# Delta rule layer: convolution sums partly in PSUM, substitution on blocks of 16 with a merge to 32 on TensorE, and compact factors for the merges

## The chip, the cores and the metric

One core of a Trainium2 chip runs the whole program. The metric is device time in microseconds (us) of one execution. TensorE (PE) does the matmuls, VectorE (DVE), ScalarE (ACT) and GpSimd (POOL) the elementwise work, and SyncE (SP) issues the DMAs.

## The reference

The network has two layers: an even one (state-space mixer and neighbourhood attention) and an odd one (gated delta rule), each with an MLP, over 128 prompt and 512 sample tokens of width 1024. The change touches the odd layer alone:

```python
def _deltanet_mixer(h, s0, w_in, conv_w, a_log, dt_bias, norm_g, w_out):
    proj = h @ w_in
    qkv = silu(_dwconv(proj[..., :3 * D_MODEL], conv_w))      # 5 taps along the tokens
    ...
    q = q * rsqrt(sum(q * q) + EPS) * DN_DK ** -0.5           # 8 heads of 128
    k = k * rsqrt(sum(k * k) + EPS)
    o_f, s_f = _gdn_chunked(q, k, v, g[:, :, 0], beta[:, :, 0], s0[:, 0])
    o_b, s_b = _gdn_chunked(q[:, ::-1], k[:, ::-1], ...)      # backward direction
    o = _rmsnorm(o_f + o_b[:, ::-1], norm_g) * silu(z)
    return o @ w_out, ...

def _gdn_chunked(q, k, v, g, beta, s0):
    a_mat = tril_strict((kb @ k.T) * decay)
    t_mat = triangular_solve(eye + a_mat, eye)                # inverse of a unit triangle
    u_c, w_c = t_mat @ (v * beta), t_mat @ (kb * exp(gcum))
    def step(s, xs):                                          # chunk after chunk
        v_new = u_i - w_i @ s
        o = (q_i * exp(g_i)) @ s + at_i @ v_new
        s = s * exp(g_last) + (k_i * exp(g_last - g_i)).T @ v_new
```

## The kernel before, in words

Features lie on the 128 partitions and the 640 tokens along the free axis. A matrix product of the network is `gemm`: for each 128 outputs it takes 2 halves of 320 tokens, and for each of the 8 input tiles three matmuls (lines 205 to 207: the weight split into a high part `whi` and a low part `wlo`, the input likewise), 24 matmuls to a half. ACT makes `whi` (line 194), POOL the difference `wlo` (line 196).

The odd layer (`odd`) works on pairs of heads, four of them. For each pair:

1. `gdn_project` runs a gemm of six output tiles m (k of two heads, q of two heads, v of two heads). Its function `ev` copies each half to a buffer `cb` (tag `cb`, two buffers; the prompt's 128 and the sample's 512 tokens with zeros between), and after the second half does the convolution on one tile `cv` of 642 columns: ACT writes the first tap (line 1319), DVE adds the four others (line 1322), ACT takes the tanh (line 1328), and a product gives silu (lines 1335 and 1336 on DVE; for the two q tiles lines 1331 to 1333 on ACT and POOL). For the v tiles of pairs 1 to 3 the last tap is done by ACT and POOL (lines 1325 and 1326). `squares` (line 1272), `tok` (line 1299) and `normalize` (line 1285) then send `cv` through TensorE, each into a PSUM bank of the tag `pc`, which has two banks.
2. `gdn_group`, for each of 5 chunks of 128 tokens, builds the triangles of two heads and two directions and writes them to DRAM (`ud`). Their 32x32 diagonal blocks, 80 of them, are gathered in a tile `ub`, one block on each of 80 partitions.
3. `gdn_blocks` inverts the 80 blocks in place by 31 substitution steps on DVE, each a product (line 1425) and a subtraction (line 1427). The result goes to DRAM (`dd`).
4. `gdn_inverse` reads it back (`gcm`), spreads it by a mask on POOL (line 1453) to block-diagonal 128x128 tiles `gD` and, transposed on DVE (line 1454), `gTT`; then merges 32x32 to 64x64 to 128x128 inverses by small matmuls (line 1458) with 128 rows and 32 or 64 columns, and ACT copies between.
5. `gdn_chain` runs the recurrence over the chunks: lines 1615, 1625, 1631, 1632 and 1643 are its matmuls of each step, 1620 and 1646 its DVE steps, and line 1567 multiplies the decayed q on POOL.

In the code a pair's steps 4 and 5 stand after the next pair's projection, with a higher priority; the last pair's stand beside the gemm of z (`zproj`, its `ev` at lines 1721 to 1724). A scheduler of the framework sets the order on each engine from these priorities when the program is built; each engine then runs its list in order, and waits on semaphores. After the layer come modulation vectors (line 281), the gating of the outputs (`gated`) and the output gemm.

Of the kernel before, what the change touches and what calls it, by code (L numbers as in the profile page):

```python
# [20 lines left out]
T = 640  # L21
# [127 lines left out]
class Build:  # L149
# [1098 lines left out]
    def gdn_project(self, pr, hn, P, first=None, mid=None):  # L1248
# [45 lines left out]
        def tok(ty):  # L1294
            for part in range(3):
# [7 lines left out]
                if part < 2:  # L1303
                    nc.scalar.activation(dst[part][:, 1:5], pv, AF.Copy)
                else:
                    for hh in range(2):
                        V.tensor_copy(dst[hh][:, 0], pv[:, hh])
        def ev(m, h, p):
# [9 lines left out]
            cv = self.tl([128, 642], "cv")  # L1318
            nc.scalar.activation(cv, cb[m][:, 0:642], AF.Identity, scale=cw[:, 0:1])  # L1319
            split = m > 3 and pr > 0  # L1320
            for t in range(1, 4 if split else 5):
                V.scalar_tensor_tensor(cv, cb[m][:, t:t + 642], cw[:, t:t + 1], cv, op0=M, op1=AD)  # L1322
            if split:
                cy = cb[m][:, 4:646]
                nc.scalar.activation(cy, cy, AF.Identity, scale=cw[:, 4:5])
                nc.gpsimd.tensor_tensor(cv, cv, cy, op=AD)
            th = cb[m][:, 0:642]
            nc.scalar.activation(th, cv, AF.Tanh)

            if m in (2, 3):  # L1330
                nc.scalar.activation(th, th, AF.Identity, bias=1.0)
                nc.gpsimd.tensor_tensor(cv[:, 0:128], th[:, 0:128], cv[:, 0:128], op=M)
                nc.gpsimd.tensor_tensor(cv[:, 128:T], th[:, 130:642], cv[:, 130:642], op=M)
            else:
                V.scalar_tensor_tensor(cv[:, 0:128], th[:, 0:128], 1.0, cv[:, 0:128], op0=AD, op1=M)
                V.scalar_tensor_tensor(cv[:, 128:T], th[:, 130:642], 1.0, cv[:, 130:642], op0=AD, op1=M)
# [78 lines left out]
    def gdn_blocks(self, pr, ub, P):  # L1415

        nc = self.nc
        V = nc.vector
        D = ub
        V.memset(D.rearrange("p a b -> p (a b)")[:, 0:1024:33], 1.0)  # L1420
        tmp = P.tile([80, 256], F32, name="sbt", bufs=1)
        for j in range(31):
            n, m = 31 - j, j + 1
            t = tmp[:, :n * m].rearrange("p (a b) -> p a b", b=m)
            V.tensor_tensor(t, ub[:, j, j + 1:32].unsqueeze(2).to_broadcast([80, n, m]),
                            D[:, j, 0:m].unsqueeze(1).to_broadcast([80, n, m]), op=ALU.mult)
            V.tensor_tensor(D[:, j + 1:32, 0:m], D[:, j + 1:32, 0:m], t, op=ALU.subtract)
            if j < 30:
                tmp = P.tile([80, 256], F32, name="sbt", bufs=1)
        dd = self.dp.tile([20, 4, 1024], F32, name="dd", tag="dd", bufs=2)  # L1430
        nc.sync.dma_start(out=dd.rearrange("a b c -> (a b) c"), in_=D.rearrange("p a b -> p (a b)"))
        return dd

    def gdn_inverse(self, pr, ud, dd, P):
# [3 lines left out]
        cm = P.tile([128, 20, 32], F32, name="gcm")  # L1438
        nc.sync.dma_start(out=cm, in_=self.ap(dd, 0, [[32, 128], [4096, 20], [1, 32]]))
# [5 lines left out]
        mask = self.cst[:, 404:532].rearrange("p (b j) -> p b j", b=4).unsqueeze(1).to_broadcast([128, 2, 4, 32])  # L1445

        D = P.tile([128, 5, 4, 128], F32, name="gD")
        TT = P.tile([128, 5, 4, 128], F32, name="gTT", bufs=2)
        two = lambda t, c, d: t[:, c, 2 * d:2 * d + 2].rearrange("p u j -> p (u j)")
        for c in range(5):  # L1450
            for d, a, b in ((0, D, TT), (1, TT, D)):
                src = cm[:, 4 * c + 2 * d:4 * c + 2 * d + 2].unsqueeze(2).to_broadcast([128, 2, 4, 32])
                G.tensor_tensor(a[:, c, 2 * d:2 * d + 2].rearrange("p u (b j) -> p u b j", b=4), src, mask, op=ALU.mult)
                V.transpose(two(b, c, d), two(a, c, d))
        CH = [(c, hh) for c in range(5) for hh in range(2)]

        def mm(out, l, r, col):
            nc.tensor.matmul(out, l, r, start=True, stop=True, tile_position=(0, col))

        def bank(n):  # L1460
            return self.ps("pb")[:, :320].rearrange("p (c h j) -> p c h j", c=5, h=2)


        p = bank(0)
        for c, hh in CH:
            for a in (0, 64):
                x, y = slice(a, a + 32), slice(a + 32, a + 64)
                mm(p[y, c, hh], uo[:, 0, c, hh, a:a + 32], D[:, c, hh, x], a + 32)
                mm(p[x, c, hh], uo[:, 1, c, hh, a:a + 32], D[:, c, 2 + hh, y], a)
        X = cm[:, :10].rearrange("p (c h) j -> p c h j", c=5)  # L1470
        ACT.activation(X, p, AF.Copy)
        pD, pT = bank(0), bank(0)
        for c, hh in CH:
            mm(pD[32:64, c, hh], TT[:, c, hh, 32:64], X[:, c, hh], 32)
            mm(pD[64:96, c, hh], TT[:, c, 2 + hh, 64:96], X[:, c, hh], 64)
        ACT.activation(D[32:64, :, 0:2, 0:32], pD[32:64], AF.Copy, scale=-1.0)
        ACT.activation(D[64:96, :, 2:4, 96:128], pD[64:96], AF.Copy, scale=-1.0)
# [11 lines left out]
        Y = cm.rearrange("p (c h a) j -> p c h (a j)", c=5, h=2)
        parts = ((0, 4), (4, 5))  # L1490
        for c0, c1 in parts:
            p = self.ps("pb").rearrange("p (c h j) -> p c h j", c=4, h=2)
            for c in range(c0, c1):
                for hh in range(2):
                    mm(p[y, c - c0, hh], uo[:, 0, c, hh, 32:96], D[:, c, hh, x], 64)
                    mm(p[x, c - c0, hh], uo[:, 1, c, hh, 0:64], D[:, c, 2 + hh, y], 0)
            ACT.activation(Y[:, c0:c1], p[:, :c1 - c0], AF.Copy)
        for c0, c1 in parts:
            p = self.ps("pb").rearrange("p (c h j) -> p c h j", c=4, h=2)
            for c in range(c0, c1):  # L1500
                for hh in range(2):
                    mm(p[x, c - c0, hh], Y[:, c, hh], TT[:, c, hh, y], 0)
                    mm(p[y, c - c0, hh], Y[:, c, hh], TT[:, c, 2 + hh, x], 64)
            ACT.activation(TT[x, c0:c1, 0:2, y], p[x, :c1 - c0], AF.Copy, scale=-1.0)
            ACT.activation(TT[y, c0:c1, 2:4, x], p[y, :c1 - c0], AF.Copy, scale=-1.0)
# [16 lines left out]
    def gdn_chain(self, pr, pd, TT, P, roles, bank):  # L1522
# [14 lines left out]
        def load(c):  # L1537

            if c not in held:
# [3 lines left out]
                held[c] = [a[k][:, i] for k in range(2) for i in range(4)]  # L1543
# [454 lines left out]
```

## Time and profile before

| what | value |
|---|---|
| median of 3 runs | 1980.04 us (1975.23 to 1983.87) |
| profiled execution | 1976.35 us, of which the span from first to last instruction is 1974.1 us |
| PE busy | 1799.6 us, 91% of the span |
| DVE busy | 1290.8 us, 65% |
| ACT busy | 869.5 us, 44% |
| POOL busy | 760.8 us, 39% |
| mean granted TensorE clock | 0.963 of full speed |

Busy time is the union of an engine's instruction spans; the odd layer takes about 900 to 1470 us of the span. The granted clock is a mean over the two levels of TensorE, 1.2 and 2.4 GHz, so 0.91 of a stretch means that a part of it ran at the lower level. Two of the profile's views are used by stretch: busy time of each engine, and the waits of an engine with what ended them.

### The profile page before, as it was taken

The page shows a single profiled execution, that of the slowest core. Times are in us where ns is not written, and L with a number is a line of the kernel's source. Part 1 is how long each engine was busy: PE and PEld are TensorE (multiplying, and loading weights), DVE is VectorE, ACT ScalarE, POOL GpSimd, SP SyncE. Part 2 cuts the span into 40 slices and gives each one's busy share as a digit, 9 for nine tenths or more (in the row PEclk, how much of TensorE's full clock was granted, in tenths as well). Part 3 has the DMA queues.
Part 4 walks back from the last instruction along what each step waited for, and adds up shares of the span by engine and source line. Part 5 has one row for each costly group of instructions (what it writes and reads, how often), then busy time and mean ns, then how long its engine had stood idle before and what let it go on. Part 6 is the DMA issues. An engine that isn't in the chain of part 4 may idle for free. (4 is left out here: it accounts for less than half of the span.)

```text
span 1974.1 us, 35755 instructions
## 1 busy us (share of the span) xinstructions
PE 1799.6 (91%) x13556; PEld 1698.3 (86%) x13556; DVE 1290.8 (65%) x2825; ACT 869.5 (44%) x1928; POOL 760.8 (39%) x609
## 2 busy tenths in 40 slices
PE   5889889998999999998877889889989899999998
PEld 3789677988999999998877788787878899999997
DVE  8999777369264544548589988774667927364553
ACT  4333356344244353536454455344324425344362
POOL 2622101442343433453455555522235334343451
PEclk9999999998999999998998999898989999999999
DMA  8446886524332222332576478758834122222231
GB/s 319 131 112 169 239 246 228 195 106 140 124 112 84 76 86 75 135 123 78 158 207 196 117 197 238 222 166 267 279 131 149 54 97 76 86 76 86 76 96 54
DMA packets 206985, 286.61 MB, mean 145 GB/s; under 512 B 54879, under 2 KB 138237, under 8 KB 206813
## 3 DMA queue, kind: packets, MB, share of 16 engines
q1 hardware_dynamic: 206812, 284.33, 45.6%
q8 instruction: 107, 1.75, 0.4%
q14 instruction: 66, 0.53, 0.1%
HBM read 228.87 MB, written 46.82 MB: 140 GB/s over the span
## 5 line engine op out<-in xcount | busy, mean ns | idle before, releaser
L196 POOL TENSOR_TENSOR wlo<-raw,whi 128x1024 fp32r<-128x1024 f32 (+1 forms) x153 | 360.8, 2361 | 512.6 <-ACT whi L194 466.6
L194 ACT ACTIVATE whi<-raw 128x1024 fp32r<-128x1024 f32 (+1 forms) x153 | 153.2, 1002 | 324.5 <-PE pg L206 146.6
L207 PE MATMUL pg<-hidh,wlo 128*128 128x320 f32 (+2 forms) x576 | 178.8, 311 | 0.5 <-POOL wlo L196 0.5
L205 PE MATMUL pg<-hidh,whi 128*128 128x320 f32 (+2 forms) x576 | 179.0, 311 | 0.0
L206 PE MATMUL pg<-hidl,whi 128*128 128x320 f32 (+2 forms) x576 | 178.9, 311 | 0.0
L205 PE MATMUL pg<-h10h,whi 128*128 128x320 f32 x472 | 158.9, 337 | 17.5 <-DVE cb L1722 6.5
L422 DVE SCALAR_TENSOR_TENSOR x<-pg,mod,x 128x128 f32<-128x128 f32 (+2 forms) x132 | 53.7, 436 | 179.5 <-PE pg L207 179.5
L206 PE MATMUL pg<-h10l,whi 128*128 128x320 f32 x472 | 155.9, 330 | 0.0
L207 PE MATMUL pg<-h10h,wlo 128*128 128x320 f32 x472 | 155.3, 329 | 0.0
L205 PE MATMUL pa<-hidh,whi 128*128 128x320 f32 x448 | 138.0, 310 | 0.5 <-ACT whi L194 0.5
L207 PE MATMUL pa<-hidh,wlo 128*128 128x320 f32 x448 | 138.4, 309 | 0.0
L206 PE MATMUL pa<-hidl,whi 128*128 128x320 f32 x448 | 138.2, 309 | 0.0
L422 DVE SCALAR_TENSOR_TENSOR x<-pa,mod,x 128x128 f32<-128x128 f32 (+2 forms) x108 | 43.8, 435 | 136.8 <-PE pa L207 136.8
L507 POOL TENSOR_TENSOR wq<-S,wq 128x512 fp32r<-128x512 f32 x52 | 71.3, 1371 | 114.4 <-ACT wq L506 114.4
L205 PEld LDWEIGHTS pg<-h10h,whi 128*128 128x128 f32 x472 | 95.9, 203 | 21.4 <-DVE cb L1722 7.2
L207 PEld LDWEIGHTS pg<-hidh,wlo 128*128 128x128 f32 x576 | 108.2, 188 | 1.6 <-POOL wlo L196 1.0
L205 PEld LDWEIGHTS pg<-hidh,whi 128*128 128x128 f32 x576 | 108.3, 188 | 0.9 <-issue 0.8
L206 PEld LDWEIGHTS pg<-hidl,whi 128*128 128x128 f32 x576 | 108.2, 188 | 0.4 <-DVE hidl L568 0.3
L1322 DVE SCALAR_TENSOR_TENSOR cv<-cb,cw,cv 128x642 f32<-128x642 f32 x90 | 94.6, 1052 | 9.8 <-ACT cv L1319 8.9
L206 PEld LDWEIGHTS pg<-h10l,whi 128*128 128x128 f32 x472 | 95.9, 203 | 0.6 <-issue 0.4
L207 PEld LDWEIGHTS pg<-h10h,wlo 128*128 128x128 f32 x472 | 95.6, 203 | 0.2
L205 PEld LDWEIGHTS pa<-hidh,whi 128*128 128x128 f32 x448 | 83.9, 188 | 2.0 <-ACT whi L194 1.2
(742 smaller groups left out, 5754.2 us busy)
## 6 DMA issues: line engine op xcount, KB each, us to landing
raw<-in_wff SPq DMA_DIRECT2D x104, 512.0 KB
mraw<-in_wmod SPq DMA_DIRECT2D x96, 512.0 KB
raw<-in_wino SPq DMA_DIRECT2D x33, 512.0 KB
rawx<-in_wff SPq DMA_DIRECT2D x24, 512.0 KB
raw<-in_wine SPq DMA_DIRECT2D x16, 512.0 KB
cka<-pd SPq DMA_DIRECT2D x28, 256.0 KB
ckb<-pd SPq DMA_DIRECT2D x28, 256.0 KB
s5g<-s5g SPq DMA_DIRECT2D x32, 164.0 KB
```

The source lines that it names most:

```text
L194: nc.scalar.activation(hi[:, :kt], raw[:, :kt], AF.Copy)
L196: (nc.vector if self.lov and self.nw % self.lov else nc.gpsimd).tensor_tensor(lo[:, :kt], raw[:, :kt], hi[:, :kt], op=ALU.subtract)
L205: nc.tensor.matmul(p[:, :n], hi[:, k], xh[:, s], start=(k == 0), stop=False)
L206: nc.tensor.matmul(p[:, :n], hi[:, k], xl[:, s], start=False, stop=False)
L207: nc.tensor.matmul(p[:, :n], lo[:, k], xh[:, s], start=False, stop=(k == kt - 1))
L422: nc.vector.scalar_tensor_tensor(x[m][:, s], p[:, ls], g, x[m][:, s], op0=ALU.mult, op1=ALU.add)
L507: (V if j % 2 else nc.gpsimd).tensor_tensor(t[:, 4:8], src, t[:, 0:4], op=SU)
L1322: V.scalar_tensor_tensor(cv, cb[m][:, t:t + 642], cw[:, t:t + 1], cv, op0=M, op1=AD)
```

## The change

- The convolution is a function `conv`. The prompt's 128 columns stay in `cv`; the sample's 512 columns are summed in a PSUM bank of the tag `pc`. Every step is done twice, once for each part. The products of the q tiles and the last tap of the v tiles go from POOL and ACT to DVE, for all pairs.
- The substitution works on blocks of 16: 15 steps, each on the two 16x16 diagonal blocks of a 32x32 block at once, into a tile `ubd` of its own that POOL clears. `ub` has one buffer in place of two.
- The pieces are read back compactly: `gDc` and `gTc` (32 rows on each of four partition groups), `gGc` (the 16x16 off-diagonal pieces, zero elsewhere), in 4 + 8 DMAs a pair in place of one. A first merge from 16 to 32 is new: two rounds of 80 matmuls of 32x32 with tile positions of row and column (line 1463), an ACT copy, a subtraction and two transposes on DVE. The later merges use the same compact factors: matmuls read 32 or 64 rows in place of 128. ACT copies the pieces to `TT` and `D64`, which POOL clears. The mask on POOL and the 40 transposes on DVE are gone.
- In the chain the decayed q is multiplied by DVE, two products of 256 columns in place of four of 128 on POOL.
- Buffers after the layer take tags that still exist (`gTT`, `gDc`), and the modulation weights alternate between `ub` and `ubd`.

```diff
+        def conv(x, cw):
+            cv = self.tl([128, 642], "cv")
+            cl = self.ps("pc")
+            parts = ((cv[:, 0:128], 0), (cl, 130))
+            for o, c0 in parts:
+                nc.scalar.activation(o, x[:, c0:c0 + o.shape[1]], AF.Identity, scale=cw[:, 0:1])
+            for t in range(1, 5):
+                for o, c0 in parts[::-1]:
+                    V.scalar_tensor_tensor(o, x[:, c0 + t:c0 + t + o.shape[1]], cw[:, t:t + 1], o, op0=M, op1=AD)
+            for o, c0 in parts[::-1]:
+                nc.scalar.activation(x[:, c0:c0 + o.shape[1]], o, AF.Tanh)
+            for (o, c0), c1 in zip(parts[::-1], (128, 0)):
+                V.scalar_tensor_tensor(cv[:, c1:c1 + o.shape[1]], x[:, c0:c0 + o.shape[1]], 1.0, o, op0=AD, op1=M)
+            return cv
...
+            cv = conv(cb[m], cw)
...
-        for j in range(31):
-            n, m = 31 - j, j + 1
...
+        D = P.tile([80, 32, 32], F32, name="ubd", bufs=1)
+        nc.gpsimd.memset(D, 0.0)
+        nc.gpsimd.memset(D.rearrange("p a b -> p (a b)")[:, 0:1024:33], 1.0)
+        def both(t, i, n, j, m):
+            return bass.AP(tensor=t.tensor, offset=t.offset + 32 * i + j, ap=[list(t.ap[0]), [528, 2], [32, n], [1, m]])
+        for j in range(15):
+            n, m = 15 - j, j + 1
+            sh = [80, 2, n, m]
+            t = P.tile([80, 128], F32, name="sbt", bufs=1)[:, :2 * n * m].rearrange("p (s a b) -> p s a b", s=2, b=m)
+            V.tensor_tensor(t, both(ub, j, 1, j + 1, n).rearrange("p s a b -> p s b a").to_broadcast(sh),
+                            both(D, j, 1, 0, m).to_broadcast(sh), op=ALU.mult)
+            V.tensor_tensor(both(D, j + 1, n, 0, m), both(D, j + 1, n, 0, m), t, op=ALU.subtract)
...
-                G.tensor_tensor(a[:, c, 2 * d:2 * d + 2].rearrange("p u (b j) -> p u b j", b=4), src, mask, op=ALU.mult)
-                V.transpose(two(b, c, d), two(a, c, d))
...
+        V.transpose(fl(Tc[:, 0]), fl(Dc[:, 0]))
+        V.transpose(fl(Dc[:, 1]), fl(Tc[:, 1]))
+        def mm(out, l, r, row, col):
+            nc.tensor.matmul(out, l, r, start=True, stop=True, tile_position=(row, col))
...
+        for d in range(2):
+            for n in range(10):
+                for r in S:
+                    mm(px[d][r, n], Gc[r, d, n], Dc[r, d, n], r.start, r.start)
+            ACT.activation(Xc[:, d], px[d], AF.Copy)
+        px = [bank() for d in range(2)]
+        for d in range(2):
+            for n in range(10):
+                for r in S:
+                    mm(px[d][r, n], Tc[r, d, n], Xc[r, d, n], r.start, r.start)
+            V.tensor_tensor(Dc[:, d], Dc[:, d], px[d], op=ALU.subtract)
+            V.transpose(fl(Tc[:, d]), fl(Dc[:, d]))
+        G.memset(D64, 0.0)
+        G.memset(TT, 0.0)
...
-                for u in range(4):
-                    nc.gpsimd.tensor_tensor(gq[:, u], gq[:, u], lds[u][2 + u % 2], op=M)
+                for d in range(2):
+                    V.tensor_tensor(gq[:, 2 * d:2 * d + 2], gq[:, 2 * d:2 * d + 2], lds[2 * d][8], op=M)
```

Since the scheduler lists every engine anew, the order moves as well. On DVE, where the substitution of the first pair begins, the list before holds the full-width steps of `cv` and the growing steps on `ub` (a row is line, operation, output<-inputs, shape):

```order
L1425 TENSOR_TENSOR sbt<-ub 80x31
L181 TENSOR_TENSOR l2n_t<-l2n_t,l2n_h 128x10
L1427 TENSOR_TENSOR ub<-ub,sbt 80x31
L182 SCALAR_TENSOR_TENSOR l2n_y<-l2n_t,l2n_y 128x10
L1425 TENSOR_TENSOR sbt<-ub 80x60
L1278 TENSOR_TENSOR ktok<-ktok,l2n_y 128x640 x2
L1427 TENSOR_TENSOR ub<-ub,sbt 80x30x2
L1425 TENSOR_TENSOR sbt<-ub 80x87
L1322 SCALAR_TENSOR_TENSOR cv<-cb,cw,cv 128x642
L1427 TENSOR_TENSOR ub<-ub,sbt 80x29x3
```

and after the change the same place on DVE holds the halved blocks and the split convolution:

```order
L1428 TENSOR_TENSOR sbt<-ub,ubd 80x30
L1322 SCALAR_TENSOR_TENSOR cv<-cb,cv 128x128
L1318 SCALAR_TENSOR_TENSOR pc<-cb,cw,pc 128x512
L1430 TENSOR_TENSOR ubd<-ubd,sbt 80x2x15
L1428 TENSOR_TENSOR sbt<-ub,ubd 80x56
L1430 TENSOR_TENSOR ubd<-ubd,sbt 80x2x14x2
L1428 TENSOR_TENSOR sbt<-ub,ubd 80x78
L1318 SCALAR_TENSOR_TENSOR cv<-cb,cw,cv 128x128
L1430 TENSOR_TENSOR ubd<-ubd,sbt 80x2x13x3
```

The steps on blocks end at 128 elements where they ended at 256, and the convolution's 642 columns have become 512 and 128. On PE the merges of the first pair stand behind 594 of the 1968 matmuls of the layer's gemms (before: behind 921), with the new level in front:

```order
L1463 MATMUL pb<-gDc,gGc 32x32 x40
L1463 MATMUL pb<-gXc,gTc 32x32 x80
L1272 MATMUL pc<-cst,tsq 128x2
L1463 MATMUL pb<-gDc,guf 32x32
L1272 MATMUL pc<-cst,tsq 128x2 x2
L206 MATMUL pg<-h10l_8974,whi 128x320
L207 MATMUL pg<-h10h_8973,wlo 128x320
L205 MATMUL pg<-h10h_8975,whi 128x320
```

The last pair's chain begins on PE behind 1704 of these matmuls, where it began behind 1584, so that 96 of them stand beside it, where 208 did, and in its last step no gemm is left between its matmuls. Before, the last step on PE reads

```order
L1625 MATMUL pb<-cR,gTT 128x128 x4
L1631 MATMUL pb<-cgq,cS 128x128
L205 MATMUL pg<-ozh_15958,whi 128x320
L206 MATMUL pg<-ozl_15959,whi 128x320
L207 MATMUL pg<-ozh_15958,wlo 128x320
```

and with the change

```order
L291 MATMUL pc<-cst,mrow 128x128 x2
L1674 MATMUL pb<-cR,ckd 128x128 x4
L1646 MATMUL pb<-cS,cka 128x128 x4
L1656 MATMUL pb<-cR,gTT 128x128 x4
L1662 MATMUL pb<-cgq,cS 128x128
L1663 MATMUL pb<-cbc,cR 128x128
```

so the matmuls of the output gemm that stood inside the step (15 of them before its second part) have moved out of it.

## Rows read from the trace of the kernel before

**Rows 1.** Busy time by engine in the layer's three stretches, then PEclk, DMA.
```profile
900.00:1000.00 100.00, 85.44 (x554) 83.63 (x553) 71.42 (x107) 55.17 (x111) 47.59 (x59) 0.91 0.47 146
1000.00:1250.00 250.00, 210.49 (x1855) 200.51 (x1853) 226.80 (x475) 129.15 (x293) 143.65 (x145) 0.91 0.69 192
1250.00:1470.00 220.00, 198.84 (x1904) 179.41 (x1905) 130.56 (x387) 83.58 (x195) 67.74 (x84) 0.95 0.69 219
```
**Rows 2.** Waits of PE from 1000 to 1250 us: total, times, longest.
```profile
PE pc L1299 <- DVE cv L1336: 6.7, 2, 6.3
PE pg L205 <- ACT cb L1316: 5.2, 4, 3.0
PE pb L1458 <- DVE gD L1454: 4.8, 6, 1.5
PE pa L1570 <- DVE otok L1600: 4.2, 1, 4.2
```
**Rows 3.** Waits of PE from 1250 to 1470 us.
```profile
PE pg L205 <- DVE cb L1722: 6.5, 2, 6.2
...
PE pb L1458 <- DVE gD L1454: 1.4, 2, 1.0
```
**Rows 4.** Groups by line, 900 to 1600 us: count, busy us, mean ns.
```profile
L1322 DVE SCALAR_TENSOR_TENSOR cv<-cb,cw,cv 128x642 f32<-128x642 f32 x90 | 94.6, 1052 | 9.8 <-ACT cv L1319 8.9 <-DMA pd<-khT 0.5
...
L1427 DVE TENSOR_TENSOR ub<-ub,sbt 80x31 f32<-80x31 f32 (+15 forms) x124 | 72.5, 584 | 1.6
L1425 DVE TENSOR_TENSOR sbt<-ub 80x31 f32<-80x31 f32 (+15 forms) x124 | 65.2, 526 | 3.0 <-DMA ub<-utd 1.2
...
L1567 POOL TENSOR_TENSOR cgq<-cgq,cka 128x128 f32<-128x128 f32 x64 | 31.5, 519 | 82.5 <-DVE cgl L1565 50.1 <-DMA cka<-pd 19.3 <-DVE ogn_t L180 7.6
...
L1453 POOL TENSOR_TENSOR gTT<-gcm,cst 128x256 f32<-128x256 f32 x20 | 18.7, 936 | 0.0
...
L1400 DVE TENSOR_TENSOR gau<-pb,gbg 128x512 f32<-128x512 f32 x20 | 13.4, 681 | 5.5 <-ACT gbg L1379 4.9 <-DMA ckb<-pd 0.6
...
L1333 POOL TENSOR_TENSOR cv<-cb,cv 128x512 f32<-128x512 f32 x8 | 12.0, 1501 | 0.0
...
L1336 DVE SCALAR_TENSOR_TENSOR cv<-cb,cv 128x512 f32<-128x512 f32 x16 | 11.1, 697 | 0.0
...
L1454 DVE STREAM_TRANSPOSE gD<-gTT 128x256 f32<-128x256 f32 x20 | 8.6, 428 | 0.5 <-POOL gTT L1453 0.5
...
L1335 DVE SCALAR_TENSOR_TENSOR cv<-cb,cv 128x128 f32<-128x128 f32 x16 | 4.5, 284 | 1.6 <-ACT cb L1328 1.3
...
L1486 ACT ACTIVATE gTT<-pb 32x320 f32<-32x320 f32 x8 | 3.4, 429 | 0.1
```
**Rows 5.** Groups by line of POOL over the whole span.
```profile
L972 POOL MEMSET qz<- 64x640 f32 x4 | 2.5, 628 | 54.5 <-DMA s5o<-yd 27.9 <-PE pc L993 19.1 <-PE pg L207 7.4
```
**Rows 6.** Order of time on DVE: start, length; two substitution steps of one size.
```profile
1032.53 2.37 DVE L1425 TENSOR_TENSOR sbt<-ub 80x175 f32<-80x175 f32 x1
...
1035.22 0.32 DVE L1427 TENSOR_TENSOR ub<-ub,sbt 80x175 f32<-80x175 f32 x1
```
**Rows 7.** Order of time on PE: a merge's matmuls (x counts passes), and eight full passes.
```profile
1122.27 0.87 PE L1458 MATMUL pb<-gTT,gcm 128*32 128x32 f32 x76
1123.07 0.83 PE L1272 MATMUL pc<-cst,tsq 128*128 128x2 f32 x6
...
1138.12 1.05 PE L1395 MATMUL pb<-khT 128*128 128x128 f32 x8
```
**Rows 8.** Order of time on PE: hand-overs inside the chains.
```profile
1388.70 1.06 PE L1615 MATMUL pb<-cS,cka 128*128 128x128 f32 x8
...
1390.97 1.16 PE L1625 MATMUL pb<-cR,gTT 128*128 128x128 f32 x8 [0.18 <-DVE cR L1620]
...
1398.91 1.06 PE L1643 MATMUL pa<-cR,ckd 128*128 128x128 f32 x8
...
1400.83 0.49 PE L1615 MATMUL pa<-cS,cka 128*128 128x128 f32 x2 [0.27 <-DVE cS L1646]
```

More of the change, by code (lines that the diff above doesn't have):

```diff
@@ L1317, in ev @@
             cw = self.cw[:, 6 * pr + m]
[L1318 to L1336, printed above, removed]
+            cv = conv(cb[m], cw)
             out[m] = cv
@@ L1455, in gdn_inverse @@
[L1455 to L1465, printed above, removed]
+        D64 = P.tile([128, 10, 64], F32, name="gD64")
+        fl = lambda t: t.rearrange("p n j -> p (n j)")
+        V.transpose(fl(Tc[:, 0]), fl(Dc[:, 0]))
+        V.transpose(fl(Dc[:, 1]), fl(Tc[:, 1]))
@@ new lines, in mm, with bank @@
+        def mm(out, l, r, row, col):
+            nc.tensor.matmul(out, l, r, start=True, stop=True, tile_position=(row, col))
+        def bank():
+            return self.ps("pb")[:, :320].rearrange("p (n j) -> p n j", n=10)
+        S = [slice(32 * k, 32 * k + 32) for k in range(4)]
+        px = [bank() for d in range(2)]
[4 more added lines that the diff above has]
+            ACT.activation(Xc[:, d], px[d], AF.Copy)
@@ new lines, in gdn_inverse @@
+        px = [bank() for d in range(2)]
+        for d in range(2):
[6 more added lines that the diff above has]
+        G.memset(TT, 0.0)
+        u2 = lambda d: slice(2 * d, 2 * d + 2)
+        ch = lambda t: t.rearrange("p (c h) j -> p c h j", h=2)
@@ L1466, in gdn_inverse @@
+        for d in range(2):
+            for r in S:
+                ACT.activation(TT[r, :, u2(d), r], ch(Tc[r, d]), AF.Copy)
+            for k in range(2):
+                r = S[2 * d + k]
+                ACT.activation(D64[r, :, 32 * k:32 * k + 32], Dc[r, d], AF.Copy)
+        p = bank()
+        for n in range(10):
+            c, hh = divmod(n, 2)
             for a in (0, 64):
                 x, y = slice(a, a + 32), slice(a + 32, a + 64)
-                mm(p[y, c, hh], uo[:, 0, c, hh, a:a + 32], D[:, c, hh, x], a + 32)
@@ L1476, in gdn_inverse @@
-        ACT.activation(D[32:64, :, 0:2, 0:32], pD[32:64], AF.Copy, scale=-1.0)
-        ACT.activation(D[64:96, :, 2:4, 96:128], pD[64:96], AF.Copy, scale=-1.0)
-        for c, hh in CH:
+        pD, pT = bank(), bank()
+        for n in range(10):
+            mm(pD[32:64, n], Tc[32:64, 0, n], X[32:64, n], 32, 32)
+            mm(pD[64:96, n], Tc[64:96, 1, n], X[64:96, n], 64, 64)
+        ACT.activation(D64[32:64, :, 0:32], pD[32:64], AF.Copy, scale=-1.0)
+        ACT.activation(D64[64:96, :, 32:64], pD[64:96], AF.Copy, scale=-1.0)
@@ L1486, in gdn_inverse @@
-            ACT.activation(TT[y, :, 2:4, x], pT[y], AF.Copy, scale=-1.0)
+            ACT.activation(TT[x, :, 0:2, y], ch(pT[x]), AF.Copy, scale=-1.0)
+            ACT.activation(TT[y, :, 2:4, x], ch(pT[y]), AF.Copy, scale=-1.0)
         x, y = slice(0, 64), slice(64, 128)
[L1489 to L1505, printed above, removed]
+        Y = Xc.rearrange("p d n j -> p (d n j)").rearrange("p (n j) -> p n j", n=10)
@@ new lines, in gdn_inverse @@
+        parts = ((0, 8), (8, 10))
+        for n0, n1 in parts:
+            p = self.ps("pb").rearrange("p (n j) -> p n j", n=8)
+            for n in range(n0, n1):
+                c, hh = divmod(n, 2)
+                mm(p[y, n - n0], uo[x, 0, c, hh, 32:96], D64[x, n], 0, 64)
+                mm(p[x, n - n0], uo[y, 1, c, hh, 0:64], D64[y, n], 64, 0)
+            ACT.activation(Y[:, n0:n1], p[:, :n1 - n0], AF.Copy)
+        for n0, n1 in parts:
+            p = self.ps("pb").rearrange("p (n j) -> p n j", n=8)
+            for n in range(n0, n1):
+                c, hh = divmod(n, 2)
+                mm(p[x, n - n0], Y[y, n], TT[y, c, hh, y], 64, 0)
+                mm(p[y, n - n0], Y[x, n], TT[x, c, 2 + hh, x], 0, 64)
+            ACT.activation(TT[x, n0 // 2:n1 // 2, 0:2, y], ch(p[x, :n1 - n0]), AF.Copy, scale=-1.0)
+            ACT.activation(TT[y, n0 // 2:n1 // 2, 2:4, x], ch(p[y, :n1 - n0]), AF.Copy, scale=-1.0)
```

55 lines of the change are left out of this document (23 added, 32 removed).

## The prediction

> **What bounds the kernel now.** I read first the busy time by engine, then the same by stretches of the odd layer, then PE's waits in each stretch, then the groups by line, and last the order of time at a few places. The whole program is a TensorE program: PE is busy 91% of the span. The change touches only the odd layer, about 900 to 1470 us. There the reader is to see that PE's idle time is not spread evenly [rows 1]: in the middle stretch, 1000 to 1250 us, PE is busy 210.5 of 250 us, so 39.5 us are lost (15.8%), while DVE is busy 226.8 us, 91%. In the last stretch DVE is at 59% and PE loses 21.2 of 220 us (9.6%). The granted clock goes along: 0.91 of 2.4 GHz in the middle, 0.95 in the last. The named waits say who is late: nearly all of the middle stretch's end with DVE or with an ACT copy into `cb` that itself waits for the convolution to give the buffer back [rows 2]. So the middle stretch is bound by DVE and PE in turn, and the rest by PE. What the change is worth is DVE time in the middle stretch, less what it adds to PE.
>
> **DVE, step by step.** The substitution is 248 instructions and 137.7 us [rows 4]. It becomes 15 steps x 2 x 4 pairs = 120. The elements of a step go from 176 on the mean to 91. One step runs clean at 0.32 us for 175 elements, and another of the same size takes 2.37 us [rows 6]: the difference is a wait inside the instruction. At today's mean price of a step of this smaller size I estimate 0.43 us, at a clean one 0.24 us, so 29 to 52 us; I take 45 and so 93 us saved. The convolution is now 90 + 32 instructions, 94.6 + 11.1 + 4.5 = 110 us [rows 4]. It becomes 24 tiles x 5 steps x two parts. No row shows a step that reads and writes PSUM; the nearest is 128x512 from PSUM at 0.681 us, and the 128-column part is 0.284 us [rows 4]. 120 x 0.965 = 116 us, so 6 more; at half the fixed cost it would be some 15 less. The decayed q costs DVE 32 products of 256 columns; the nearest two rows, 0.284 us for 128 columns and 0.697 for 512, bracket it at about 0.43, so 14 us. The 40 transposes at 0.428 us, of which one group of two is shown, go (17 us); 16 of 320 columns come at an estimated 0.5 (8 us), and 8 subtractions from PSUM at about 0.5 (4 us). Sum: -93 + 6 + 14 - 17 + 8 + 4 = -78 us of 429, with bounds of about -60 and -105.
>
> The Trainium skill (SBUF — State Buffer, "Reading the diagram" of the port model) says that VectorE and GpSimd share a port pair as an exclusive lock, and that a VectorE instruction with two SBUF inputs blocks against a GpSimd one that reads SBUF. The 2.37 us above agrees with it, since a clean step takes 0.32 us. By that rule a convolution step with its sum in PSUM has one SBUF tensor input and would always run clean, while the rows' mean of today's step is 1.052 us for 642 columns; no run here shows it yet.
>
> **POOL and ACT.** POOL loses the 64 products of q (31.5 us), the 40 masks (18.7 us for twenty, the other twenty alike) and the products on the q tiles (12.0 us and a smaller part) [rows 4], and gains four memsets a pair: 1024 + 640 + 640 + 2560 columns at 0.628 us per 640 [rows 5], 4.8 us a pair. It falls by some 60 to 75 us of 259. ACT gains 14 copies a pair at 0.43 us [rows 4], 24 us, and pays its convolution steps twice, for some 7 us; the scaling and the +1 passes that it sheds give about 11 back. With 268 us busy in 570 [rows 1] that is covered by its idle time; should ACT be late, the evictions into `cb` would hold PE, which costs what the 5.2 us of [rows 2] cost now. SP issues 11 more DMAs a pair, all beside the substitution's read-back; they land some us later than one DMA would, while PE works through gemms, and if that cover fails the chain only starts later.
>
> **PE: what is added.** The merges of a pair are now 140 matmuls, that is 280 passes in the trace (each fp32 matmul shows as two). They become 300, that is 600 passes; the 320 extra ones are 32 columns wide. Today 76 passes of that width, four column tiles side by side, start within 0.80 us [rows 7], so 10.5 to 13 ns each. At 12.7 ns the extra cost is 4.1 us a pair and 16 us in all. The other bound is from the full passes: eight of 128 columns start at 0.11 us intervals (1.05 us less the pipeline's tail of about 0.2, by seven) [rows 7], so a 32-column pass without any overlap costs about a quarter, 28 ns, and the extra ones 36 us; if the older merges lost their overlap too, about 47 us. Nothing is no bound, since every pass has to be issued. The new level looks like the old ones, neighbours in four different tiles, so I take 16.
>
> The Trainium skill speaks against this (TensorEngine Tiling (Array Packing), "Gotcha 1: PSUM Pressure"): different row tiles cannot access the same PSUM bank at once, and here the four row tiles of a group all write one bank. By it the extra passes would cost the unoverlapped 36 us and not 16; no row of this trace has a row-tiled matmul, so it is a rival below.
>
> **PE: what goes.** In the middle stretch 4.8 us of waits for transposed `gD` tiles go for good [rows 2], since no transposes alternate with matmuls any more. Of the other waits I let most go, because their releasers are DVE instructions queued behind 100 us of substitution: DVE falls from 227 to about 170 us there, 72% of a shorter stretch. I take two thirds of the 39.5 us: -26 us; bounds 0 and -36. The clock: at 0.93 in place of 0.91, half way to the next stretch's 0.95, PE's 210 us shrink by 4.5 us; bounds 0 and 9. In the last stretch 6.5 us of PE's wait for the z tiles' DVE step and 1.4 us for `gD` [rows 3] fall in the time of the last substitution; -6 us. From 900 to 1000 us DVE is at 71% with convolutions alone, whose DVE time hardly changes: 0.
>
> **PE: the tail.** The last pair's chain now has 96 gemm matmuls beside it, where it had 208. A step's hand-overs take 2.27 us (first matmuls to second), 1.92 us (last to the next step's first) [rows 8] and a third like them, about 2.0, with 1.8 us of output matmuls between, so 8 us a step, of which PE works about 5. Uncovered, each step costs 3 us. The modulation matmuls still cover the first two; I add 4 us, with bounds of 0 and 12.
>
> Sum: -26 - 4.5 - 6 + 16 + 4 = -16.5 us. Against the profiled execution's own 1976.35 us, which is 3.7 us under the median of the runs shown, this gives 1960 us.
>
> **Rivals.**
> 1. *PE does not get what DVE gives back.* From 900 to 1000 us DVE is at 71%, where I expect it in the middle, and PE idles 14.6% all the same, at a clock of 0.91 [rows 1]. PE's waits would then be the latency of chains (PE, ACT, DVE, PE), not DVE's queue. With 14.6% idle the middle stretch gains 3 us, the last 3, and PE pays 16 + 4: 1990 us, slower. It decides where less than half of the 39.5 us goes (1976 - 20 - 3 + 20). Against it: the longest waits there [rows 2] are single ones behind DVE's backlog, 6.3 of 6.7 us at once, which is no latency.
> 2. *The PSUM bank.* `conv` holds one of two `pc` banks from its first ACT step to its last product: 0.6 + 4 x 0.68 + 0.6 + 0.68, about 5 us clean and 7 with other work between, six times a pair; PE needs 11 banks a pair of that tag for squares and transposes. If each of the 44 waits 1 us more, 1960 + 44 = 2004 us, slower. It tips the sign at 0.4 us each. The order on PE for it: such matmuls stand between gemms, so PE's whole list waits. Against it: the scheduler knows the banks and has placed them later.
> 3. *Row tiles do not overlap* (the rule above): 36 us and not 16 for the new level, 1980 us; with the older merges 1991 us.
> 4. *All of it comes out*: waits of 36 us gone, clock 0.95, last stretch 8: -53 + 16 + 4, so 1943 us; with half the price of the passes and a covered tail 1931 us.
>
> **How the numbers follow.** About 0.5%, 10 us, is what a measurement of this kernel can tell from no change. I give the forecast 0.48 (1945 to 1975 us), rival 4 0.12, rival 1 0.20, rival 2 0.12 and rival 3 0.08. The range for 8 in 10 reaches from 1930 (rival 4's end) to 1993 us (rivals 1 and 3); rival 2's larger values and the combinations stay out. Faster by over 0.5%, under 1966.5: four fifths of the forecast, all of rival 4 and a little of rivals 1 and 3, 0.55. Within: the forecast's upper end, a third of rival 1 and half of rival 3, 0.21. Slower: most of rivals 1 and 2, some of 3, 0.24.
>
> **What would show it.** In the changed kernel's profile: substitution near 45 us in 120 instructions; DVE in the layer at about 350 us; 2400 passes of merges with a PE busy time near 45 us (rival 3: 65 or more); PE's idle time over the layer near 50 us in place of 75, the wait for `gD` gone (rival 1: the same idle, other releasers); few waits of squares or transposes for `pc` banks (rival 2: tens of us under lines 1272, 1285 and 1299); a granted clock of 0.93 or more between the first and the last convolution; and the last chain's steps some 8 us apart with short waits between. The prediction is wrong if DVE's time falls as worked out and PE's idle time does not, or if the new matmuls take twice their price.

## The result, and the profile after

The changed kernel takes 2027.14 us (median of 4 runs, 2024.37 to 2034.64) and the kernel before 1978.55 us: ratio 1.0248, 95% interval 1.0227 to 1.0269. It is 49 us slower, where 1960 us was forecast. The profiled execution has a span of 2023.5 us, 49.4 more than before, and a mean granted clock of 0.949 (before 0.963). From the page of the changed kernel, busy time by engine (PEld is TensorE's loading of weights, which overlaps PE):

```profile
PE 1819.5 (90%) x14836; PEld 1713.7 (85%) x14836; DVE 1233.2 (61%) x2827; ACT 890.0 (44%) x2018; POOL 670.2 (33%) x503
```

PE is busy 19.9 us longer, and its idle time (span less busy) went from 174.5 to 204.0 us, up 29.5. DVE lost 57.6 us, POOL 90.6 (60 to 75 were forecast). So the work went where it was meant to go, and PE did not get the time. The stretches that answer to [rows 1], and the one behind them, since the layer now ends later:

```profile
900.00:1000.00 100.00, 75.75 (x451) 72.01 (x450) 70.33 (x122) 46.54 (x108) 42.08 (x48) 0.84 0.49 144
1000.00:1250.00 250.00, 206.68 (x2441) 196.33 (x2440) 171.09 (x465) 128.60 (x321) 73.06 (x93) 0.86 0.62 172
1250.00:1470.00 220.00, 193.43 (x2392) 180.50 (x2391) 109.87 (x310) 100.01 (x231) 46.83 (x35) 0.91 0.65 202
1470.00:1540.00 70.00, 54.82 (x389) 45.52 (x388) 34.61 (x106) 18.21 (x42) 16.88 (x13) 0.85 0.51 168
```

In the middle stretch DVE fell from 226.8 to 171.1 us, yet PE idles 43.3 us there, 3.8 more than before, and the clock is 0.86 in place of 0.91. From 900 to 1000 us, where nothing was expected, PE lost 9.7 us. The largest waits of PE, 900 to 1650 us (total, times, longest):

```profile
PE pb L1394 <- DVE gau L1399: 15.2, 5, 6.8
PE pc L1285 <- DVE ktok L1278: 8.3, 4, 6.7
PE pc L1272 <- ACT tsq L1268: 7.8, 7, 2.5
PE pa L1700 <- DVE osc L1697: 7.3, 1, 7.3
PE pb L1463 <- DVE gDc L1481: 6.7, 2, 6.2
PE pb L1463 <- DVE gau L1399: 5.7, 4, 2.2
```

The waits for `cb` and for `cv` of [rows 2, 3] are gone from the head of the list. In their place stand `gdn_group`'s products of `khT` with itself (L1394), which wait for DVE to give a `pb` bank back, and the new merges (L1463). The groups that answer to [rows 4], on DVE, 900 to 1650 us:

```profile
L1318 DVE SCALAR_TENSOR_TENSOR pc<-cb,cw,pc 128x512 f32<-128x512 f32 x96 | 70.2, 747 | 14.5 <-ACT pc L1315 14.0
L1318 DVE SCALAR_TENSOR_TENSOR cv<-cb,cw,cv 128x128 f32<-128x128 f32 x96 | 50.1, 522 | 8.8 <-ACT cv L1315 7.6
L1430 DVE TENSOR_TENSOR ubd<-ubd,sbt 80x30 f32<-80x30 f32 (+7 forms) x60 | 20.7, 344 | 1.0
L1428 DVE TENSOR_TENSOR sbt<-ub,ubd 80x30 f32<-80x30 f32 (+7 forms) x60 | 18.7, 312 | 12.7 <-DMA ub<-utd 9.8 <-issue 2.0
L1598 DVE TENSOR_TENSOR cgq<-cgq,cka 128x256 f32<-128x256 f32 x32 | 17.8, 568 | 13.2 <-DMA cka<-pd 13.2
L1322 DVE SCALAR_TENSOR_TENSOR cv<-cb,pc 128x512 f32<-128x512 f32 x24 | 16.1, 677 | 4.6 <-ACT cb L1320 4.6
L1322 DVE SCALAR_TENSOR_TENSOR cv<-cb,cv 128x128 f32<-128x128 f32 x24 | 11.6, 482 | 4.0 <-ACT cb L1320 4.0
```

The substitution is 39.4 us, the convolution 148.0.

### The profile page after: what moved, and what is told of

It is laid out like the page before. It is cut to its first block, busy times and chain, and to the rows that moved or that the text cites. A ratio compares the mean times of both kernels' runs of the same rounds, so it can differ in the third digit from the quotient of the medians.

```text
span 2023.5 us, 38356 instructions
## 1 busy us (share of the span) xinstructions
PE 1819.5 (90%) x14836; PEld 1713.7 (85%) x14836; DVE 1233.2 (61%) x2827; ACT 890.0 (44%) x2018; POOL 670.2 (33%) x503
## 3 DMA queue, kind: packets, MB, share of 16 engines
q8 instruction: 117, 1.92, 0.4%
## 4 chain that ended last, share of the span: by engine, by line
PE 57%; DVE 16%; DMA 15%; issue 5%; SPq 4%; ACT 2%; POOL 2%; POOLq 0%; DVEq 0%; ACTq 0%
PE pg L205 7%; PE pg L206 7%; PE pg L207 7%; PE pa L206 5%; PE pa L205 4%; PE pa L207 4%; PE pg L525 2%; PE pg L527 2%; PE pg L526 2%; DMA utd<-gut 2%; PE pa L525 2%; PE pb L525 2%; PE pa L527 2%; PE pb L527 2%; PE pa L526 2%
## 5 line engine op out<-in xcount | busy, mean ns | idle before, releaser
L196 POOL TENSOR_TENSOR wlo<-raw,whi 128x1024 fp32r<-128x1024 f32 (+1 forms) x153 | 355.1, 2324 | 642.2 <-ACT whi L194 592.0
L207 PEld LDWEIGHTS pa<-hidh,wlo 128*128 128x128 f32 x448 | 84.0, 188 | 0.4 <-issue 0.4
```

The lines of the kernel that those rows point to most:

```text
L196: (nc.vector if self.lov and self.nw % self.lov else nc.gpsimd).tensor_tensor(lo[:, :kt], raw[:, :kt], hi[:, :kt], op=ALU.subtract)
L207: nc.tensor.matmul(p[:, :n], lo[:, k], xh[:, s], start=False, stop=(k == kt - 1))
```

## The experiments

All ratios stand against runs of the kernel before on the same chip, whose median there lies between 1977 and 1981 us; medians of two runs that are set against each other below can carry up to 4 us of that difference. The letters of the theories are those of the expectations. First, which part.

**The new convolution alone on the kernel before.**

```diff
-            cv = self.tl([128, 642], "cv")
...
+            cv = conv(cb[m], cw)
```

> The kernel before with the new convolution alone (sum of the sample's columns in a PSUM bank, all products on DVE); substitution, merges and the chain's q product stay as before. Theory A (the loss comes with the blocks of 16, the new merge level and where PE's list then puts the dependent short matmuls): within 10 us of the kernel before, 1970 to 1990 us. Theory B (the convolution is the cause: its DVE groups took 120 us in place of 110 and it holds a pc bank): most of the 49 us is here, 2000 to 2030 us.

1987.6 us, ratio 1.0043 (1.0026 to 1.0059). (The 120 us that the expectation names are the adding steps alone, which were 94.6; with the products the convolution takes 148 us in the changed kernel, where it took 110.)

**The changed kernel with the convolution of before**, the same edit backwards.

> The changed kernel with the convolution of before; blocks of 16, new merges and q product on DVE stay. Theory A: still slow, 2005 to 2035 us. Theory B: 1970 to 1990 us.

1992.3 us, 1.0061 (1.0043 to 1.0078).

**The same, and the q product on POOL.**

```diff
-                    V.tensor_tensor(gq[:, 2 * d:2 * d + 2], gq[:, 2 * d:2 * d + 2], lds[2 * d][8], op=M)
+                    nc.gpsimd.tensor_tensor(gq[:, u], gq[:, u], lds[u][2 + u % 2], op=M)
```

> The changed kernel with the convolution and the q product of before: the blocks of 16 and the new merges are all that is left. Theory A: 2005 to 2035 us, as the run that keeps the q product on DVE, within 8 us. Theory B: 1970 to 1990 us. Theory C (the q product on DVE makes the chains wait in DVE's queue): 10 us or more below the run that keeps it there.

1995.4 us, 1.0071 (1.0054 to 1.0089).

**The changed kernel with the q product on POOL alone.**

> The changed kernel with the chain's q product back on POOL, all else as changed. Theories A and B: within 8 us of the changed kernel, 2019 to 2035 us. Theory C: 10 us or more below it, under 2017 us.

2015.8 us, 1.0178 (1.0161 to 1.0195). Neither theory A nor B holds whole. The convolution alone costs 8 us, the blocks and merges 16, together (with q on POOL) 36. Moving q costs 11 us in the one pair of kernels and gives 3 in the other, so it has no sign of its own.

Next, what of the convolution hurts beside the new merges: the split steps or the bank.

**The sample's sum in SBUF.**

```diff
-            cl = self.ps("pc")
+            cl = cv[:, 130:642]
```

> The changed kernel with one line other: the convolution's 512 sample columns are summed in SBUF (in cv) and no longer in a pc bank; the steps stay split in two parts, all else as changed. Theory P (the bank: each convolution queues for one of two pc banks behind the transposes of the tiles before it, and the scheduler's list then holds the gemm at the tile's boundary and packs all the chunks' products kT x kT there, so that PE waits): it falls to the run that has the convolution of before, 1985 to 2000 us. Theory S (the split convolution's DVE time, 120 us and more, is what hurts): 2012 us or more, since the DVE work is the same or more.

1997.1 us, 1.0087 (1.0072 to 1.0102), as theory P had it: one line gives 30 us back, though DVE is busy 23 us longer (1256.3 us). PE is idle 21.8 us less (182.2 us) and busy 6.5 us less (1813.0 us).

**The PSUM sum for the v tiles alone** (`m > 3`).

> The changed kernel with the PSUM sum for the two v tiles of a pair alone, in SBUF for the k and q tiles. Theory P: the bank is held where no normalize follows, so near the run with no PSUM sum, 1985 to 2003 us. Theory S: as the changed kernel, 2012 us or more.

2002.5 us, 1.0108 (1.0091 to 1.0125), just inside theory P's bounds.

**The kernel before with an unused bank held.**

```diff
+            cl = self.ps("pc")
+            nc.scalar.activation(cl[:, 0:2], cb[m][:, 0:2], AF.Copy)
             nc.scalar.activation(cv, cb[m][:, 0:642], AF.Identity, scale=cw[:, 0:1])
...
+            V.tensor_copy(cb[m][:, 0:2], cl[:, 0:2])
```

> The kernel before, in which each convolution takes a pc bank and holds it from its first step to its last without using it: ACT copies two columns into it ahead of the first tap, DVE copies them back behind the product. Nothing else changes. Theory P: this alone costs what the new convolution alone cost, some 8 us: 1984 to 1996 us. Theory S: no change, 1975 to 1983 us.

1979.1 us, 0.9996 (0.9983 to 1.0009): no cost.

**The same bank in the changed kernel without its convolution.**

> The changed kernel with the convolution of before (1992 us without more), in which each convolution holds an unused pc bank as in the run above. Theory P: 2010 to 2030 us, near the changed kernel. Theory S: 1988 to 1998 us.

2006.4 us, 1.0134 (1.0111 to 1.0156): 14 us over the run without the bank, between the bounds of the two theories. So the bank costs nothing on the kernel before, 14 us beside the new merges when only held (no more than the order alone moves such a kernel, as the last runs show), and 30 when the sum is in it.

Where it shows: in PE's list all ten products of `khT` of the first pair stand in one place, with no gemm between, in the five kernels that sum all tiles in PSUM, and PE waits at these products for 16 to 19 us in all, 890 to 1650 us. With the sum in SBUF they are spread over 36 gemm matmuls, before over 40, and in every other kernel the wait is 1 to 11 us. The row of the changed kernel stands above (15.2); the same row with the sum in SBUF:

```profile
PE pb L1394 <- DVE gau L1399: 3.5, 2, 1.8
```

At these products and at the merges together PE waits 42.3 us in the changed kernel and 17.5 with the sum in SBUF, a difference of 24.8 us. That the packed order sets the 30 us is argued, and it is not the whole: the new convolution alone on the kernel before has the same order and 28.9 us of these waits, where the kernel before has 14.7, and costs 8 us. The held bank has no such order; there PE is busy 14.2 us longer (1827.1 us, at a mean clock of 0.949 in place of 0.960) and idle 6.2 us less. The order of time in the changed kernel at the second pair, on PE, then POOL, ACT and DVE:

```profile
1045.50 2.08 PE L1394 MATMUL pb<-khT 128*128 128x128 f32 x8 [1.13 <-DVE gau L1399]
1053.16 1.22 PE L1394 MATMUL pb<-khT 128*128 128x128 f32 x4 [5.59 <-DVE gau L1399]
...
1049.76 1.26 POOL L1375 TENSOR_TENSOR gbg<-gbg,cst 128x512 f32<-128x512 f32 x1 [2.96 <-DMA gbg<-gbd]
...
1051.05 1.28 ACT L1378 ACTIVATE gbg<-gbg,ngc 128x128 f32<-128x128 f32 x4 [7.70 <-POOL gbg L1375]
...
1052.42 0.69 DVE L1399 TENSOR_TENSOR gau<-pb,gbg 128x512 f32<-128x512 f32 x1 [2.75 <-ACT gbg L1378]
```

Read from the bottom: PE waits for the `pb` bank, DVE's product for the decay from ACT, ACT for POOL's mask, POOL for a DMA into `gbg`, of which there are two buffers for five chunks. The chain's instructions were there before too; gemms stood between the products.

Then, whether DVE's relief is worth anything, and what the level from 16 to 32 costs.

**The first 15 of 31 substitution steps on the kernel before.**

```diff
-        for j in range(31):
+        for j in range(15):
```

> The kernel before with the first 15 of the 31 substitution steps alone; the other 16 are left out (so part of each 32x32 inverse is not computed). DVE loses about half of its 137.7 us of substitution and nothing is added anywhere. Theory G (as predicted: PE's idle time in the middle of the layer is DVE's backlog, two thirds of it go): 1950 to 1962 us. Theory L (PE's waits there are latencies of short dependent chains and head-of-line waits in PE's list, which stay when DVE is freed): 1972 to 1983 us.

1959.9 us, 0.9913 (0.9890 to 0.9936): theory G. DVE lost 47.8 us, and the time fell 17.

**Blocks of 16 and compact merges without the level.** The two rounds between `px = [bank() ...` and `G.memset(D64, 0.0)` are cut from the run at 1995 us.

> The changed kernel with convolution and q product of before (1995 us), without the merge from 16 to 32: its 160 matmuls a pair, two ACT copies, the subtractions and two transposes are left out (the off-diagonal 16x16 pieces of the inverse are not computed). DVE stays relieved by some 70 us. Theory G: 1950 to 1962 us, the relief without the price. Theory L: 1973 to 1985 us, that is the price of the new level, 13 us of PE's busy time and a few us of hand-overs, comes off and nothing more.

1952.4 us, 0.9875 (0.9851 to 0.9900): theory G again. The level costs 43 us. The pages' busy rows without and with it:

```profile
PE 1792.6 (92%) x13556; PEld 1694.7 (87%) x13556; DVE 1218.2 (63%) x2661; ACT 888.3 (46%) x1976; POOL 735.1 (38%) x589
```
```profile
PE 1818.8 (91%) x14836; PEld 1714.3 (86%) x14836; DVE 1215.5 (61%) x2677; ACT 894.2 (45%) x1984; POOL 732.0 (37%) x589
```

1280 more passes, 26.2 us more of PE busy (18.8 in the merges' own lines, 22.80 to 41.64; the other 7.4 go along with a lower clock, 0.957 over the span for 0.963) and, the spans being 1948.1 and 1990.0, 15.7 us more idle.

**The changed kernel without the level.**

> The changed kernel without the level from 16 to 32 (its 160 matmuls a pair, copies, subtractions and transposes left out, so the off-diagonal 16x16 pieces of the inverse are not computed); the convolution keeps its PSUM bank. If level and bank add up: 2027 less 43 is 1984 us, that is 32 us over the run without either. If the bank costs only what it did on the kernel before (8 us for the whole new convolution): 1957 to 1965 us.

1978.3 us, 0.9987 (0.9970 to 1.0003). The level costs 49 us here; convolution, bank and q together cost 26 without it. Level and bank add up, within 6 us of the first value expected. It divides as above: the merges' own lines are busy 18.8 us longer with the level (28.44 to 47.20), and PE is idle 22.7 us longer (181.3 to 204.0).

**Compact merges on blocks of 32.**

> The kernel before with the compact merges alone: substitution on blocks of 32 as before (31 steps, into a cleared tile), no merge from 16 to 32, no mask on POOL and no 40 transposes; convolution and q product as before. The whole result is computed. The waits for gD (6 us) go, PE's work stays. Theory L: 1968 to 1982 us, no worse than the kernel before, at best by the waits for gD. Theory M (the compact read-back in many small DMAs and the ACT copies into TT and D64 are a cost of their own): 1985 us or more.

1995.8 us, 1.0091 (1.0061 to 1.0120). It falls to theory M by the bounds, but the same read-back and copies stand in the run at 1952 us; what makes it 19 us slower than before is open.

**The level's matmuls issued and unread.**

```diff
-            ACT.activation(Xc[:, d], px[d], AF.Copy)
...
-                    mm(px[d][r, n], Tc[r, d, n], Xc[r, d, n], r.start, r.start)
-            V.tensor_tensor(Dc[:, d], Dc[:, d], px[d], op=ALU.subtract)
-            V.transpose(fl(Tc[:, d]), fl(Dc[:, d]))
+                    mm(px[d][r, n], Tc[r, d, n], Gc[r, d, n], r.start, r.start)
```

> As the run without the level from 16 to 32 (1952 us), but with that level's 160 matmuls a pair issued in their place, both rounds on data that is ready, and their results left unread: no copy, no subtraction, no transposes between (so the off-diagonal 16x16 pieces are not computed). Theory K (the passes and what they do to PE's list and clock make up the level's 43 us): 1985 to 1998 us. Theory H (the hand-overs PE to ACT to PE to DVE and back make up what is over the 19 us by which PE's busy time in the merges rose): 1966 to 1978 us.

2021.8 us, 1.0221 (1.0194 to 1.0248), above both theories: without any hand-over it is dearer than with them. But PE's list had changed as well, and its waits in the chains are 39 us, where the run without the level has 14; so the run decides for neither theory, and what the hand-overs cost stays open.

**The same number of matmuls behind the last chain.**

```diff
+        for i in range(4):
+            for q in range(4):
+                px = self.ps("pb")[:, :320].rearrange("p (n j) -> p n j", n=10)
...
+                        nc.tensor.matmul(px[r, n], self.ident[r, 0:32], self.ident[r, 32:64], start=True, stop=True, tile_position=(32 * k, 32 * k))
```

> The run without the level (1952 us) with as many matmuls of 32x32 (640, on constants, results unread) in two blocks behind the layer's last chain, where nothing waits for them; PE's list ahead of them does not change. It prices the passes alone. Theory K1 (1280 passes by themselves take PE's time and slow its clock behind them): 1985 us or more. Theory K2 (a pass is worth 10 to 15 ns, and the rest of the level's 43 us comes from where the list puts the level and the chains around it): 1964 to 1974 us.

1993.5 us, 1.0077 (1.0060 to 1.0094): theory K1, 41 us for 1280 passes that wait for nothing and that nothing waits for. Most of it can be seen in the order of time on PE, where 1200 of them stand in one line (the 181 passes just ahead of these rows start without a gap):

```profile
1440.09 1.93 PE L1793 MATMUL pb<-cst 32*32 32x32 f32 x128 [2.62 <-issue]
1443.56 1.93 PE L1793 MATMUL pb<-cst 32*32 32x32 f32 x128 [1.54 <-issue]
1447.31 1.93 PE L1793 MATMUL pb<-cst 32*32 32x32 f32 x128 [1.82 <-issue]
1450.78 1.93 PE L1793 MATMUL pb<-cst 32*32 32x32 f32 x128 [1.54 <-issue]
1454.52 1.93 PE L1793 MATMUL pb<-cst 32*32 32x32 f32 x128 [1.81 <-issue]
```

Bursts of 128 passes, each begun some 3.6 us after the last (14.43 us for four): 28 ns a pass. Between them PE waits 1.5 to 2.6 us for no engine and no DMA of the program. The DMA queues of that kernel, 1430 to 1470 us (packets, MB, share), and busy time from 1436 to 1467 us:

```profile
q8 instruction: 10, 0.16, 1.8%
```
```profile
1436.00:1467.00 31.00, 16.48 (x1183) 15.47 (x1171) 1.47 (x9) 0.00 (x0) 0.00 (x0) 0.56 0.02 5
```

One instruction packet of 16 KB goes with each burst (10 for 1280 passes; of the three from 1440 to 1451 us, each lies within a burst and none in a gap). That the gaps are PE waiting for its instructions is inferred from this; no run changed the supply. The matmuls are busy 18.0 us, the gaps take 14.5, and the granted clock is 0.56 over the stretch, at the lower level from 1440 us on, behind the first gap; a gemm matmul behind the line takes 0.47 us until 1470.5 us and 0.31 after. That is 32.5 of the 43.4 us by which the profiled span grew; the rest is 3.9 us of PE busy and 7.0 us of idle time elsewhere.

Last, how much is the order alone: the same instructions, the priority of inverse and chain changed.

```diff
-            with tc.high_priority(offset=10000):
+            with tc.high_priority(offset=1000):
```

> The run with the blocks of 16 and new merges alone (1995 us), same instructions, with the priority of the inverse and chain of the first three pairs at 1000 in place of 10000, so that the scheduler writes another order. Theory N (the order matters little, the instructions set the time): within 6 us of 1995. Theory O (a list's order alone moves this layer by 10 us and more): outside 1985 to 2005 us.

2010.2 us, 1.0152 (1.0127 to 1.0178): 15 over 1995.

> The same with that priority at 3000: PE's list differs from the run at 10000 only from the second pair's chain on. Theory N: within 6 us of 1995. Theory O: off by more than 6 us, and from the run at 1000 too.

1994.6 us, 1.0070 (1.0045 to 1.0095): no change.

> The changed kernel (2027 us), same instructions, with that priority at 1000. The chunks' products stay packed at one place of the gemm (pairs 0 and 1). Theory N and theory P (the bank): 2020 to 2034 us. Theory O: outside that.

2029.3 us, 1.0252 (1.0228 to 1.0276): no change.

> The kernel before, same instructions, with the priority of the inverse and chain of the first three pairs at 1000 in place of 10000: another list. Theory O (the order alone moves this layer by 10 us and more, and the kernel before has a good one): 1988 to 2000 us. Theory N: 1973 to 1986 us.

1983.9 us, 1.0027 (1.0010 to 1.0044): 4 more. The order alone moves these kernels by 0 to 15 us. Differences of about that size (the q product, the split steps at 5 us, the held bank's 14, the 19 of the compact merges on blocks of 32) are not taken as prices; the level (43, 49, 41 us) and the bank in the changed kernel (30 us) are larger. No kernel that computes everything beat the one before.

## Why the prediction was wrong, by its own steps

By the prediction's own sign it is wrong "if DVE's time falls as worked out and PE's idle time does not", and that came: DVE in the layer (900 to 1470 us) is 351 us, where about 350 was forecast (the layer now runs past 1470 us; over the span DVE lost 57.6 us of the 78), and PE's idle time there is 94 us, where it was 75 and near 50 was forecast. Over the whole span PE's idle time was to fall by some 28 us and rose by 29.5; PE's busy time was to rise by some 11.5 and rose by 19.9. So nearly all of the miss is idle time.

**What bounds the kernel: right, and mis-sized.** DVE's share in the middle fell to 68% of 250 us, where 72% was forecast. Relief does reach PE: half the substitution gives 17 us, the blocks with compact merges 25 (idle 174.5 to 155.5 us, PE busy 7 less). The terms for it (-26, -4.5 and -6) were 36.5 together; with nothing else in the way 25 of them came.

**PE, what is added: this step failed, by what stands around the passes.** It took 12.7 ns a pass from 76 passes that start within 0.80 us [rows 7], 16 us in all, and put nothing beside the passes for the level. The passes came out as priced. Busy time of PE and PEld at the merges' line, 880 to 1650 us, in the kernel before, the changed kernel, and the runs at 1952 us (no level) and 1995 us (with it):

```profile
880.00:1650.00 770.00, 28.67 (x1120) 22.63 (x1120) 0.93 0.55 167
880.00:1650.00 770.00, 47.20 (x2400) 40.13 (x2400) 0.89 0.54 163
880.00:1650.00 770.00, 22.80 (x1120) 19.93 (x1120) 0.94 0.57 171
880.00:1650.00 770.00, 41.64 (x2400) 35.02 (x2400) 0.92 0.55 166
```

The prediction's sign was near 45 us for 2400 passes (rival 3: 65 or more); it is 47.2. With and without the level the difference is 18.8 us, 14.7 ns a pass. But the level costs 43 us in that pair: on top of the 18.8, PE is idle 15.7 us longer, and busy 7.4 us longer in other lines at a lower clock. In the changed kernel it is again 18.8, and 22.7 us of idle time. The forecast had nothing for either.

What the idle time is made of is open. Waits that end with issue, as the gaps of the long line do, are 4.1 us at the merges of the run at 1995 us and 2.8 in the changed kernel (0.3 to 13.8 in the other kernels with the level). So the price of the long line, 28 ns a pass with the gaps, is not what was paid in place: the level's rounds are 160 passes each, and such a round can run without a gap, as in the run at 1995 us (first row); a piece of the changed kernel is as fast (second row).

```profile
1076.62 1.92 PE L1465 MATMUL pb<-gXc,gTc 32*32 32x32 f32 x160
1302.61 0.81 PE L1463 MATMUL pb<-gXc,gTc 32*32 32x32 f32 x65
```

The "other bound" of 36 us had nearly the number, by another mechanism. (By its own working, 1.05 less 0.2 by seven, the interval of the full passes is 0.12 us and not 0.11, and the bound 39 us.) Rival 3 is not borne out: the 65 passes cycle over four row tiles that write one bank, and start 9.5 ns apart (0.81 less the tail of 0.2, by 64). The Trainium skill (TensorEngine Tiling (Array Packing), "Gotcha 1: PSUM Pressure") says that such tiles cannot access a bank at once; these rows show no price of it.

**The convolution's bank, costed at nothing.** This term failed too. Rival 2 had the resource right and the place wrong. It looked for waits of squares and transposes: those at lines 1272, 1285 and 1299 are some 19 us from 890 to 1650 us, and were 20 before. The cost is 30 us in the changed kernel, shown by the one-line run, and the waits that came with it stand at the chunks' products and at the merges. Why an unused bank costs 14 us beside the new merges and nothing beside the old ones is open.

**DVE's sum.** -78 was forecast, -57.6 came. The substitution was right (45 and 39.4), q near (14 and 17.8). The convolution was forecast at 116 and is 148: the 128-column part was taken at the clean 0.284 us and takes 0.522 on the mean. The two kinds of step, from the line's own view in the changed kernel (min/median/max in ns; 890 to 1320 us):

```profile
L1318 DVE SCALAR_TENSOR_TENSOR cv<-cb,cw,cv x96: 306/347/2412, 909.3 to 1282.5; 128x128 f32<-128x128 f32 x96
L1318 DVE SCALAR_TENSOR_TENSOR pc<-cb,cw,pc x92: 712/749/757, 934.7 to 1281.8; 128x512 f32<-128x512 f32 x92
```

With the sum in PSUM the longest step is 45 ns over the shortest; with it in SBUF a step of a quarter of the columns can take 2.4 us. In the run with the sample's sum in SBUF the same 512 columns take 850 ns a step on the mean, where they take 747 in the changed kernel. In the changed kernel's trace the 12 of the 96 steps of 128 columns that take over 0.5 us all lie beside a POOL instruction (memsets aside), of the other 84 seven do; 29 of the 96 steps into PSUM lie beside one too, and none is longer for it. The Trainium skill (SBUF — State Buffer, "Reading the diagram" of the port model) has it that a VectorE instruction with two SBUF inputs blocks against a GpSimd one that reads SBUF; these rows agree with it. So the bank did what it was for on DVE, and its price was paid on PE.

**The rest.** The tail's +4 was not separated by a run. The clock was 0.86 in the middle, not 0.93. Rival 1 comes nearest to the outcome, idle time that stays with other releasers, but not to its cause, since DVE's relief arrives once the level is gone; and the idle time did not stay, it rose.

Put together along the runs, from the 1977 us that the kernel before took beside the first of them: -25 for blocks and compact merges (1952.4), +43 for the level (1995.4), -3 for q (1992.3), +5 for the split steps (1997.1), +30 for the bank (2027). The forecast had -36.5, +16, 0, 0 and 0, and +4 for the tail.

## What to carry to other kernels

A price per pass is not the price of a level: here the passes cost 18.8 us where 16 was forecast, and idle time and a lower clock around them 24 us more. Before a PSUM bank is lent to a long elementwise chain, look at what the scheduler's list does with the matmuls behind it, and try the one-line version without the bank. A neighbour that is freed gives only what the added work on the bounding engine leaves: take the relief and the price in separate runs before judging the pair.

## What the runs showed of the hardware

A line of 1200 matmul passes of 32x32 in fp32 advances, behind its first 181 passes, in bursts of 128, one 16 KB instruction packet for each, 3.6 us apart, and the granted clock stayed at the lower level over these bursts and gaps; a single round of 160 passes took 1.92 us. A DVE step that sums 512 columns into PSUM hardly varies (712 to 757 ns), where one of 128 columns with two SBUF inputs takes 306 to 2412 ns.
